# Second layers of the two middle MLP parts as seven half-size products each, in one stream with the first layers

## The chip, the cores and the metric

The kernel runs on one core of one Trainium2 chip. The metric is the device time of one execution in microseconds. A core has five engines that work beside each other and wait for one another through semaphores: TensorE (PE) for matrix products, whose results go to PSUM; VectorE (DVE) and ScalarE (ACT), which read and write both PSUM and SBUF; GpSimd (POOL), which works on SBUF; and SyncE (SP), whose queue issues the transfers from and to HBM. Each engine takes its instructions in a fixed order.

## The reference, cut to what matters

One layer of an encoder for 512 prompt tokens and 64 sample tokens (576 in all), width 1024. After attention, a convolution and an output projection, an MLP with a hidden width of 4096 ends the layer; only this MLP is touched here.

```python
h = rms_norm(x, norm2_g) * (1 + sc2) + sh2
x = x + g2 * (jnp.square(jax.nn.relu(h @ w_ff1)) @ w_ff2)
...
y_prompt = rms_norm(yp, final_g)
y_sample = rms_norm(ys, final_g)
```

`w_ff1` is 1024 x 4096, `w_ff2` 4096 x 1024, all in 32-bit floats.

## The kernel before

**Number format.** A 32-bit operand is split into a high part of the type that TensorE multiplies and a low part, the rest: ACT copies the high part (`copy_to`, L106) and DVE or POOL subtracts it from the source for the low part (`sub`, L115, and L334 in `split`). One product of 128 x 128 weights with a block of tokens is three matmuls: high times high, high times low, low times high. Tokens are columns, in two halves of 288 (`JS`).

**Parts.** The hidden width is cut into four parts of 1024. For each part the first layer makes eight hidden tiles (`a`, 128 hidden rows x 576 tokens, a high and a low part each), and the second layer adds their product with 1024 rows of `w_ff2`, times the gate, onto the residual `x1` (`residual`, L1085, on DVE, straight from PSUM). Part 0's first layer is plain and also prepares the normed input; the last part's second layer is plain as well, in token ranges of 320 and 256, with the final norm behind it.

**Fast first layers.** Parts 1, 2 and 3 make their first layer with Strassen's scheme (`fast_layer`, L1371). Two hidden tiles at a time (a *pair*, `q`), the 2 x 2 blocks of weights (inner half by hidden tile) and of the input (inner half by token half) need seven half-size products instead of eight. The seven moving operands (`op`: "11", "12", "22" and four sums "s1" to "s4") are made once, during part 0's second layer (`operands`, L1294). The seven weight operands (a *block* each, 128 x 512 high and low in one buffer) are made afresh for each pair: `sums` (L1334) forms the sums of weight blocks on DVE, `block` (L1342) copies the high part on ACT and subtracts the low part on DVE (numbers 1, 4, 5) or POOL (0, 2, 3, 6). Blocks go through four buffers and are made three products ahead. A product is 12 matmuls of 288 columns. Products 0 and 2 add up in one PSUM bank, products 1, 3 and 5 in a second and 4 and 6 in a third, and the four results are formed from these banks with a few additions of DVE as the products come: `y` keeps product 0 (ACT), `u` is bank 1 + `y` after product 1, the second `y` the same after product 3, and so on. Because a later product adds onto a bank that is read in between, product 2 must wait until `y` has read bank 0, product 3 for `u`, product 5 for the second `y` and product 6 for the addition from bank 4 (L1417). `made` (L1364) then applies relu and square on ACT, in PSUM, and splits the result into `a`.

**Plain second layers.** For parts 0, 1 and 2 eight output tiles times two token halves times eight hidden tiles times three matmuls (`weight2`, `group`, `residual`; L1488 to L1503). Weights come 128 columns at a time, 512 KB a transfer, and are split by ACT and POOL.

**What sets the order.** PE, ACT, DVE and POOL run in the order in which the code emits their instructions in this stage (`manual_schedule`); the DMA queue is ordered by the scheduler. PSUM has eight banks: two (`tp`) for sums of weights and six that `p_ff` (L1233) hands out in turn. `owed` and `settle` (L1203) put a subtraction off until something later on DVE. `fetch` (L318) issues the next weight transfer, into one of three buffers (`wraw`) or a `spare` one.

Of the kernel before, what the change touches and what calls it, by code (L numbers as in the profile page):

```python
# [71 lines left out]
def step_kernel(ctx: ExitStack, tc: tile.TileContext, io):  # L72
# [240 lines left out]
    for part in range(NP_):  # L313
        order += [f_rows(w_ff1, 0, 128 * (KP * part + m)) for m in range(KP)]
        order += [f_rows(w_ff2, 128 * KP * part, 128 * m) for m in range(NK)]
    stay = []

    def fetch(home=None):  # L318
        if order:
            raw = home() if home else wgt.tile([128, 1024], FT, name="wraw", tag="wraw", bufs=3)  # L320
            src = order.pop(0)
            nc.sync.dma_start(raw.rearrange("p (k c) -> p k c", k=src.shape[1]), src)
            raws.append(raw)
# [1000 lines left out]


    pairs, blocks = {}, {}

    def bring(q):
        b0, b1 = raws.pop(0), raws.pop(0)
        x = p_tp()  # L1330
        copy_to(act, x, b1[:, :512])
        pairs[q] = [b0[:, :512], b0[:, 512:], b1[:, :512], b1[:, 512:], x]

    def sums(q, n):  # L1334

        if n == 2:
            pairs[q].append(p_tp())
        b11, b21, b12, b22, x, *y = pairs[q]
        out, u, v = ((b12, b22, x), (x, x, b11), (y and y[0], b22, x), (y and y[0], b21, y and y[0]))[n]
        sub(dve, out, u, v)  # L1340

    def block(g):  # L1342
        q, b = g // 7, g % 7
        b11, b21, b12, b22, x, y = pairs[q] if len(pairs[q]) == 6 else pairs[q] + [None]
        src = (b11, y, b21, b12, x, y, b22)[b]
# [3 lines left out]
        return lambda: sub(dve if b in (1, 4, 5) else pool, w[:, 1], src, f(w[:, 0]))  # L1349

    MOVING = ("11", "s2", "12", "s3", "s1", "22", "s4")

    def early(n):

        if n == 0:
            bring(0)
            sums(0, 0)
            sums(0, 1)
        else:
            sums(0, 2)  # L1360
            for g in range(2):
                block(g)()

    def made(q, a, r):  # L1364

        act.activation(q, q, AF.Relu)
        act.activation(q, q, AF.Square)
        copy_to(act, a[:, 0, r], q)
        owed.append(lambda: sub(dve, a[:, 1, r], q, f(a[:, 0, r])))

    def fast_layer():  # L1371
        a_ = []
        end = 7 * (KP // 2)
        bk = old = None
        for g in range(end + 2):
            q, s = g // 7, g % 7
            if s == 0:
                old, bk = bk, {}
            if g < end:
                if s in (0, 1, 4):  # L1380
                    bk[s] = p_ff()[:, :HALF]
                t = bk[(0, 1, 0, 1, 4, 1, 4)[s]]
                w, x = blocks.pop(g), ops[MOVING[s]]
                for k in range(4):
                    c = slice(128 * k, 128 * k + 128)
                    r = slice(HALF * (k % 2), HALF * (k % 2) + HALF)
                    for n, (z, y) in enumerate(((0, 0), (0, 1), (1, 0))):
                        pe.matmul(t, lhsT=w[:, z, c], rhs=x[k // 2][:, y, r], start=s in (0, 1, 4) and k + n == 0,  # L1388
                                  stop=k == 3 and n == 2, skip_group_check=True)
            if s == 1 and g < end:  # L1390
                bk["y"] = mt([128, 2, HALF], FT, "y3")
                copy_to(act, bk["y"][:, 0], bk[0])
            todo = [block(h) for h in ((2, 3) if g == 0 else (g + 3,)) if h < end]
            if s == 0 and old:
                dve.tensor_tensor(old[4], old[4], old["u"], op=OP.add)
                settle()
# [203 lines left out]
```

## Time and profile before

| | us |
|---|---|
| median of 3 runs | 837.2 (837.08 to 838.21) |
| the profiled execution | 837.84 |
| its span, first to last instruction | 836.1 |
| PE busy in the span | 784.3 (94%) |
| DVE busy | 526.7 (63%) |
| ACT busy | 465.2 (56%) |
| POOL busy | 296.8 (36%) |

The mean granted clock of TensorE was 0.977 of full speed. The MLP's second half looks like this in time (us from the span's start): the first fast layer begins at 534.7; fast layer and plain second layer of part 1 end at 630.2, those of part 2 at 725.5; part 3's fast layer ends at 769.8 and its second layer, with the final norm and the output, fills the rest. Busy times are unions: where one instruction begins before the one ahead on its engine is through, as on ACT and DVE here, the durations of the instructions add up to more than the busy time.

### The profile page before, as it was taken

Reading aid. Unit: us, or ns where it says so; the run is one execution under the profiler, and the core shown is the slowest. Engines: PE = TensorE matmul, PEld = TensorE weight load, DVE = VectorE, ACT = ScalarE, POOL = GpSimd, SP = SyncE. Lnnn points to the kernel's source line nnn. Section 1 sums busy time; section 2 is a strip of 40 time slices with the busy share of each in tenths; the row PEclk is TensorE's granted clock in tenths of the full one; section 3 lists DMA queues with packets and bytes.
Section 4 is the critical chain, followed back from the end, with each engine's and each line's share of the span. In section 5 each row is a group of like instructions: output and inputs, shape, how many; then the busy total and the mean of one; then the engine's idle time right before and its main releaser. Section 6 shows DMA issues by size and latency. Waiting matters only on the chain.

```text
span 836.1 us, 17187 instructions
## 1 busy us (share of the span) xinstructions
PE 784.3 (94%) x6643; PEld 729.7 (87%) x6643; DVE 526.7 (63%) x1234; ACT 465.2 (56%) x1104; POOL 296.8 (36%) x327
## 2 busy tenths in 40 slices
PE   4898898897889899999999999999999999999995
PEld 3697886486778788898999999999999999999995
DVE  4569879999998444464774678675226731476452
ACT  5354653555676688855465854486216741388231
POOL 1146253131244523323233354444334444344400
PEclk9799999899999999999999999999999999999999
DMA  8974248147434334654132235223322252323311
GB/s 240 322 199 118 77 115 224 53 110 193 116 90 120 93 109 116 201 164 119 52 101 60 81 89 150 79 77 101 101 77 83 55 141 77 88 69 98 101 62 53
DMA packets 164556, 95.57 MB, mean 114 GB/s; under 512 B 7699, under 2 KB 161119, under 8 KB 164475
## 3 DMA queue, kind: packets, MB, share of 16 engines
q1 hardware_dynamic: 164475, 94.48, 40.4%
q8 instruction: 52, 0.85, 0.4%
q14 instruction: 29, 0.24, 0.1%
HBM read 88.82 MB, written 5.64 MB: 113 GB/s over the span
## 4 chain that ended last, share of the span: by engine, by line
PE 67%; DVE 18%; ACT 7%; issue 4%; DMA 2%; POOL 1%; SPq 0%; ACTq 0%; DVEq 0%; POOLq 0%
PE ps_acc L290 9%; PE ps_acc L291 8%; PE ps_acc L292 8%; PE ps_acc L1388 8%; PE ps_lg L1388 4%; DVE yc L566 4%; PE ps_lg L290 3%; PE ps_lg L292 3%; PE ps_lg L291 3%; DVE score L692 3%; DVE m L690 2%; PE ps_av L1388 2%; PE ps_tp L234 2%; PE ps_av L292 2%; PE ps_av L290 2%
## 5 line engine op out<-in xcount | busy, mean ns | idle before, releaser
L334 POOL TENSOR_TENSOR wlo<-wraw,whi 128x512 fp32r<-128x512 f32 x122 | 162.6, 1351 | 271.1 <-ACT whi L106 268.4
L106 ACT ACTIVATE whi<-wraw 128x512 fp32r<-128x512 f32 x148 | 87.6, 624 | 99.5 <-issue 85.3
L290 PE MATMUL ps_acc<-h,whi 128*128 128x288 f32 (+1 forms) x416 | 133.7, 322 | 0.0
L291 PE MATMUL ps_acc<-h,whi 128*128 128x288 f32 (+1 forms) x416 | 124.4, 299 | 0.0
L292 PE MATMUL ps_acc<-h,wlo 128*128 128x288 f32 (+1 forms) x416 | 124.2, 299 | 0.0
L290 PEld LDWEIGHTS ps_acc<-h,whi 128*128 128x128 f32 x416 | 80.0, 192 | 14.3 <-issue 12.7
L291 PEld LDWEIGHTS ps_acc<-h,whi 128*128 128x128 f32 x416 | 80.0, 192 | 0.9
L292 PEld LDWEIGHTS ps_acc<-h,wlo 128*128 128x128 f32 x416 | 79.8, 192 | 0.0
L1089 DVE SCALAR_TENSOR_TENSOR x<-ps_acc,mod,x 128x288 f32<-128x288 f32 (+3 forms) x91 | 36.2, 421 | 60.4 <-PE ps_acc L292 60.0
L566 DVE SCALAR_TENSOR_TENSOR yc<-u,cw,yc 128x606 f32<-128x606 f32 x60 | 58.6, 985 | 0.6
L292 PE MATMUL ps_acc<-a,wlo 128*128 128x288 f32 x192 | 56.6, 295 | 0.0
L290 PE MATMUL ps_acc<-a,whi 128*128 128x288 f32 x192 | 56.6, 295 | 0.0
L291 PE MATMUL ps_acc<-a,whi 128*128 128x288 f32 x192 | 56.6, 295 | 0.0
L749 ACT ACTIVATE gc<-sful,sg 128x544 bf16<-128x544 f32 x48 | 35.8, 745 | 28.6 <-DVE sg L747 27.8
L115 POOL TENSOR_TENSOR whi<-wraw,whi 128x512 fp32r<-128x512 f32 x24 | 31.1, 1295 | 52.3 <-ACT whi L106 51.1
L115 POOL TENSOR_TENSOR wlo<-wraw,wlo 128x512 fp32r<-128x512 f32 x24 | 31.1, 1294 | 34.4 <-ACT wlo L106 32.5
L874 POOL TENSOR_SCALAR prob<-prob,mx 128x128 f32<-128x128 f32 (+3 forms) x32 | 20.2, 634 | 56.8 <-DVE mx L873 31.4
L1388 PE MATMUL ps_acc<-op,whi 128*128 128x288 f32 x264 | 38.5, 295 | 0.0
L1388 PE MATMUL ps_acc<-op,wlo 128*128 128x288 f32 x264 | 38.5, 295 | 0.0
L292 PE MATMUL ps_lg<-a,wlo 128*128 128x288 f32 x128 | 37.8, 295 | 0.0
L291 PE MATMUL ps_lg<-a,whi 128*128 128x288 f32 x128 | 37.7, 295 | 0.0
L290 PE MATMUL ps_lg<-a,whi 128*128 128x288 f32 x128 | 37.7, 295 | 0.0
(418 smaller groups left out, 2267.8 us busy)
## 6 DMA issues: line engine op xcount, KB each, us to landing
wraw<-w_ff SPq DMA_DIRECT2D x64, 512.0 KB
ada<-w_ada SPq DMA_DIRECT2D x44, 512.0 KB
wraw<-w_in SPq DMA_DIRECT2D x24, 512.0 KB
wraw<-w_out SPq DMA_DIRECT2D x8, 512.0 KB
rep<-ud SPq DMA_DIRECT2D x24, 115.0 KB
xtok<-x_prompt SPq DMA_DIRECT2D x4, 512.0 KB
ada<-w_ada SPq DMA_DIRECT2D x8, 256.0 KB
ct<-cache_k SPq DMA_DIRECT2D x8, 256.0 KB
```

The source lines that it names most:

```text
L106: act.activation(out, in_, AF.Copy, scale=1.0 if scale is None else scale)
L115: eng.tensor_tensor(out, a, b, op=OP.subtract)
L290: pe.matmul(out, lhsT=hi, rhs=src[:, 0, cs_], start=first, stop=False)
L291: pe.matmul(out, lhsT=hi, rhs=src[:, 1, cs_], start=False, stop=False)
L292: pe.matmul(out, lhsT=lo, rhs=src[:, 0, cs_], start=False, stop=last)
L334: behind[0] = (second[0] if c.start else pool).tensor_tensor(lo[:, c], raw[:, c], f(hi[:, c]), op=OP.subtract).ins
L566: dve.scalar_tensor_tensor(yc[c], src, w, yc[c], op0=OP.mult, op1=OP.add)
L692: last[0] = dve.match_replace(score[i], m, score[i], SENT).ins
L749: act.activation(eq, sful, AF.Sign, bias=cands[:, z:z + 1], scale=-1.0, accum_out=cnts[:, z:z + 1])
L874: pool.tensor_scalar(pt[:, :n], pt[:, :n], m[:, 1:2], 1.0, op0=OP.mult, op1=OP.mult)
L1089: dve.scalar_tensor_tensor(xm[:, a:b], t[:, a - r.start:b - r.start], mod[:, g, s, m:m + 1], xm[:, a:b], op0=OP.mult, op1=OP.add)
L1388: pe.matmul(t, lhsT=w[:, z, c], rhs=x[k // 2][:, y, r], start=s in (0, 1, 4) and k + n == 0, stop=k == 3 and n == 2, skip_group_check=True)
```

## The change

The second layers of parts 1 and 2 are made with seven half-size products as well. With the tiles of the hidden layer taken as pairs (the two hidden tiles of a pair are the two inner halves) and output tiles as pairs too, a layer has four pairs of seven products. Five layers now form one stream of products, `KINDS`: first and second of part 1 ("in", "out"), first and second of part 2, first of part 3. `line` is the order of the products, `due` a table of what each engine does during which product, `g`, sorted by a rank; `perform(g)` emits it behind the matmuls of product `g`.

The moving operands of an "out" layer are the seven blocks and sums of the squared hidden values. They are made by the "in" layer ahead of it as each pair's results leave PSUM (`evac`, `summed`): four results, of which "21" is needed only inside sums, then the sums "s1" to "s4" by DVE, and seven splits (`opa`) where there were four (`a`). Two small buffers hold values on the way (`va`, `vb`). The "in" layer of part 3 makes `a` as before. The copy `y` of product 0 moves from ACT to DVE in the "in" layers and stays on ACT in the "out" layers. In the "out" layers results go onto the residual (`onto`), eight whole or cut pieces a pair as before. In all five layers two of the four sums of weights (`sum1`, `sum3`) move from DVE to POOL, and with `sum1` in SBUF (`wsum`) also the low part of block 4: POOL has seven instructions a pair where it had four. PSUM banks are handed out by the longest free (`get_bank`, `put_bank`). The last pair of an "in" layer uses smaller delays (`hurry`), and the first two pairs of an "out" layer are interleaved (`line`), so that products come in the order in which their moving operands are made. A 512 KB transfer of `w_ff2` for these layers is issued as two of 256 KB.

```diff
+    for n, (kind, part) in enumerate(KINDS):
+        o = PAIRS * n
+        if kind == "out":
+            line += [(o, 0), (o + 1, 0), (o, 2), (o, 1), (o, 4), (o, 3), (o + 1, 2), (o, 5), (o, 6),
+                     (o + 1, 1), (o + 1, 4), (o + 1, 3), (o + 2, 0), (o + 1, 5), (o + 1, 6)]
+            line += [(o + 2, b) for b in range(1, 7)] + [(o + 3, b) for b in range(7)]
+        else:
+            line += [(o + q, b) for q in range(PAIRS) for b in range(7)]
...
+    def sum1(q):
+        bring(q)[2] = ft_([128, 512], FT, "wsum")
+        sub(pool, pairs[q][2], half_of(q, 2), half_of(q, 0))
...
+    def sum3(q):
+        b12 = half_of(q, 2)
+        sub(pool, b12, half_of(q, 3), b12)
...
-        return lambda: sub(dve if b in (1, 4, 5) else pool, w[:, 1], src, f(w[:, 0]))
+        return lambda: sub(dve if b in (1, 5) else pool, w[:, 1], src, f(w[:, 0]))
...
+    for h, (q, b) in enumerate(line):
+        g = h - 3 if h != 2 else 0
+        block_at(g, h)
+        if b == 1:
+            at(h - 6, 0, sum1, q)
+            at(h - 5, 8, sum2, q)
+            at(h - 4, 8, sum2, q)
+        if b == 3:
+            at(h - 5, 0, sum3, q)
+        if b == 5:
+            at(h - 6, 8, sum4, q)
...
+        def rise(key):
+            act.activation(k_[key], k_[key], AF.Relu)
+            act.activation(k_[key], k_[key], AF.Square)
+            if summed and key == 0:
+                k_["a"] = small_("va")
+                copy_to(act, k_["a"], k_[0])
...
+            def high():
+                if summed:
+                    to.extend(into(o, i))
...
+                copy_to(act, to[0], k_[key])
+
+            def low():
+                sub(dve, to[1], k_[key], f(to[0]))
...
+        def keep():
+            k_["y"] = mt([128, 2, HALF], FT, "y3")
+            copy_to(dve if kind == "in" else act, k_["y"][:, 0], k_[0])
...
+        def sums():
+            add(k_[5], k_[5], k_["b"])
+            sub(dve, k_["a"], k_[5], k_["a"])
...
+            if summed:
+                at(g + 2 + h, 4, sums)
+                at(g + 3 + h, 4, lambda: sub(dve, k_[0], k_[0], k_["b"]))
+                for o, key, d, e in (("s2", "a", 3 + h, h), ("s1", 5, 3 + h, 1), ("s3", 0, 4, h)):
+                    pieces(d, 5, key, o, e)
+        if b == 6:
+            at(g + 1, 0, lambda: add(k_[4], k_[4], k_["u"]))
+            result(1 + h, 4, "12")
+            if summed:
+                at(g + 3 + 3 * h, 7, lambda: sub(dve, k_[4], k_[4], k_["a"]))
+                pieces(4 + 3 * h, 5, 4, "s4")
...
-    for part in range(NP_ - 1):
-        a_ = fast_layer() if part else first_layer()
...
+    a_ = []
+    for n in range(len(KINDS)):
+        fast(PAIRS * n, a_ if n == len(KINDS) - 1 else None)
```

**TensorE, end of part 1's first layer.** `op` is a moving operand of the first layer, `opa` one made from hidden values, `a` a hidden tile; `whi` and `wlo` are weight buffers (in the fast layers a whole block stands in either). Before:

```order
L1388 MATMUL ps_acc<-op,wlo 128x288 x12
L1388 MATMUL ps_acc<-op,whi 128x288 x12
L1388 MATMUL ps_acc<-op,wlo 128x288 x12
L290 MATMUL ps_lg<-a,whi 128x288
L291 MATMUL ps_lg<-a,whi 128x288
L292 MATMUL ps_lg<-a,wlo 128x288
```

Now, from the last two products of the first layer on:

```order
L1479 MATMUL ps_acc<-op,whi 128x288 x12
L1479 MATMUL ps_lg<-op,wlo 128x288 x12
L1479 MATMUL ps_av<-opa,whi 128x288 x12
L1479 MATMUL ps_acc<-opa,wlo 128x288 x12
L1479 MATMUL ps_av<-opa,whi 128x288 x12
L1479 MATMUL ps_lg<-opa,wlo 128x288 x12
L1479 MATMUL ps_acc<-opa,whi 128x288 x12
```

Behind the first layer stand products of 12 matmuls in place of groups of 24, and the third of them adds onto the bank of the first.

**ACT, a middle pair of part 1's first layer**, from the copy of block 1's high part on. L1366/L1496 is relu, L1367/L1497 square, `y_` the copy of product 0 (its buffer numbers differ). Before:

```order
L106 ACTIVATE whi<-ps_tp 128x512
L1366 ACTIVATE ps_acc<-ps_acc 128x288
L1367 ACTIVATE ps_acc<-ps_acc 128x288
L106 ACTIVATE a<-ps_acc 128x288
L106 ACTIVATE wlo<-ps_tp 128x512
L106 ACTIVATE ps_tp<-wraw_7052 128x512
L106 ACTIVATE whi<-wraw_6906 128x512
```

Now:

```order
L106 ACTIVATE wlo<-ps_tp 128x512
L1496 ACTIVATE ps_acc<-ps_acc 128x288
L1497 ACTIVATE ps_acc<-ps_acc 128x288
L106 ACTIVATE va<-ps_acc 128x288
L106 ACTIVATE opa<-ps_acc 128x288
L106 ACTIVATE whi<-wraw 128x512
L1496 ACTIVATE ps_acc<-ps_acc 128x288
L1497 ACTIVATE ps_acc<-ps_acc 128x288
L106 ACTIVATE opa<-ps_acc 128x288
L106 ACTIVATE opa<-ps_lg 128x288
L106 ACTIVATE wlo<-wraw_6845 128x512
```

Between one block and the next, ACT now has up to four 288-wide instructions where it had at most three, or three and the copy `y`.

**DVE, middle pairs of part 1's first layer.** L1395 to L1421 and L1493 are additions, L115 a subtraction; `a<-...,a` and `opa<-...,opa` make a low part. Before, from the second `y` of a pair on (L1413):

```order
L1413 TENSOR_TENSOR y_6978<-ps_lg,y_6978 128x288
L115 TENSOR_TENSOR a<-ps_lg,a 128x288
L115 TENSOR_TENSOR ps_tp<-wraw_6906,ps_tp 128x512
L1417 TENSOR_TENSOR ps_acc<-ps_acc,y_6978 128x288
L115 TENSOR_TENSOR wlo<-ps_tp,wlo 128x512
L1421 TENSOR_TENSOR ps_lg<-ps_lg,y_6978 128x288
```

Now, from the copy of a pair's product 0 (L110) to its second `y`, in the last row:

```order
L110 COPY y_7143<-ps_av 128x288
L1493 TENSOR_TENSOR ps_acc<-ps_acc,vb 128x288
L115 TENSOR_TENSOR va<-ps_acc,va 128x288
L1493 TENSOR_TENSOR u_7173<-ps_acc,y_7143 128x288
L115 TENSOR_TENSOR opa<-ps_lg,opa 128x288
L115 TENSOR_TENSOR ps_acc<-ps_acc,vb 128x288
L115 TENSOR_TENSOR wlo<-ps_tp,wlo 128x512
L115 TENSOR_TENSOR opa<-va,opa 128x288
L115 TENSOR_TENSOR opa<-ps_acc,opa 128x288 x2
L1493 TENSOR_TENSOR y_7143<-ps_acc,y_7143 128x288
```

The second `y`, for which product 5 waits, now stands behind three low parts of sums, of which the first reads SBUF alone.

## Rows read from the trace of the kernel before

**Rows 1.** the page: busy time, share and instructions of each engine in the span

```profile
PE 784.3 (94%) x6643; PEld 729.7 (87%) x6643; DVE 526.7 (63%) x1234; ACT 465.2 (56%) x1104; POOL 296.8 (36%) x327
```

**Rows 2.** busy time by stretch: window, length, busy us (instructions) of each engine, clock, DMA

```profile
core 0: us, PE busy (x) PEld busy (x) DVE busy (x) ACT busy (x) POOL busy (x), PEclk, DMA share, GB/s
...
534.89:579.50 44.61, 44.61 (x340) 44.61 (x339) 30.90 (x60) 34.76 (x80) 20.69 (x16) 1.00 0.26 73
579.50:630.25 50.75, 50.75 (x385) 50.75 (x384) 12.57 (x30) 11.21 (x22) 19.09 (x15) 1.00 0.36 103
630.25:674.80 44.55, 44.55 (x339) 44.55 (x339) 30.84 (x60) 34.82 (x80) 20.66 (x16) 1.00 0.26 73
674.80:725.53 50.73, 50.73 (x386) 50.73 (x385) 12.61 (x30) 11.26 (x22) 19.09 (x15) 1.00 0.37 103
725.53:772.00 46.47, 46.47 (x352) 46.47 (x352) 31.48 (x63) 36.51 (x84) 20.72 (x17) 1.00 0.31 89
```

**Rows 3.** all waits of PE from 530 to 780 us: total, times, longest

```profile
PE ps_av L292 <- POOL wl L334: 0.4, 1, 0.4
```

**Rows 4.** timeline, part 2's fast layer, PE: start, length, engine, line, operation, shapes

```profile
641.19 1.75 PE L1388 MATMUL ps_acc<-op,wlo 128*128 128x288 f32 x12
...
642.78 1.75 PE L1388 MATMUL ps_acc<-op,whi 128*128 128x288 f32 x12
...
649.12 1.75 PE L1388 MATMUL ps_acc<-op,whi 128*128 128x288 f32 x12
```

**Rows 5.** timeline, the same stretch, ACT

```profile
641.20 0.41 ACT L106 ACTIVATE a<-ps_lg 128x288 fp32r<-128x288 f32 x1
...
641.50 0.62 ACT L106 ACTIVATE whi<-wraw 128x512 fp32r<-128x512 f32 x1
...
642.02 0.40 ACT L1366 ACTIVATE ps_av<-ps_av 128x288 f32<-128x288 f32 x1
...
642.46 0.40 ACT L1367 ACTIVATE ps_av<-ps_av 128x288 f32<-128x288 f32 x1
...
642.89 0.41 ACT L106 ACTIVATE a<-ps_av 128x288 fp32r<-128x288 f32 x1
643.19 0.41 ACT L106 ACTIVATE y<-ps_acc 128x288 f32<-128x288 f32 x1
```

**Rows 6.** timeline, the same stretch, DVE; in brackets its idle time before

```profile
644.30 0.68 DVE L115 TENSOR_TENSOR wlo<-ps_tp,wlo 128x512 fp32r<-128x512 f32 x1
...
644.90 0.45 DVE L1407 TENSOR_TENSOR u<-ps_acc,y 128x288 f32<-128x288 f32 x1
...
645.29 0.46 DVE L115 TENSOR_TENSOR a<-ps_lg,a 128x288 fp32r<-128x288 f32 x1
...
649.32 0.47 DVE L1417 TENSOR_TENSOR ps_av<-ps_acc,y 128x288 f32<-128x288 f32 x1 [0.16 <-PE ps_acc L1388]
```

**Rows 7.** timeline, the same stretch, POOL

```profile
642.20 1.29 POOL L115 TENSOR_TENSOR whi<-wraw,whi 128x512 fp32r<-128x512 f32 x1 [0.39 <-ACT whi L106]
```

**Rows 8.** groups of ACT in part 2's fast layer: total us, mean ns, idle before

```profile
L106 ACT ACTIVATE whi<-wraw 128x512 fp32r<-128x512 f32 x9 | 5.5, 628 | 2.8 <-PE ps_acc L1388 1.5 <-PE ps_acc L291 1.3
...
L106 ACT ACTIVATE a<-ps_acc 128x288 fp32r<-128x288 f32 x7 | 2.9, 412 | 0.2
L1366 ACT ACTIVATE ps_acc<-ps_acc 128x288 f32<-128x288 f32 x7 | 2.8, 405 | 0.0
L1367 ACT ACTIVATE ps_acc<-ps_acc 128x288 f32<-128x288 f32 x7 | 2.8, 395 | 0.2
```

**Rows 9.** DVE instructions with two SBUF inputs: min/median/max ns

```profile
L115 DVE TENSOR_TENSOR op<-full,op x16: 448/452/1557, 494.8 to 519.8; 128x288 fp32r<-128x288 f32 x16
L115 DVE TENSOR_TENSOR op<-sums,op x12: 446/456/1554, 496.7 to 524.6; 128x288 fp32r<-128x288 f32 x12
```

**Rows 10.** timeline, part 0's second layer, such instructions beside POOL

```profile
522.77 3.38 DVE L115 TENSOR_TENSOR op<-sums,op 128x288 fp32r<-128x288 f32 x3
...
522.84 3.01 POOL L334 TENSOR_TENSOR wlo<-wraw,whi 128x512 fp32r<-128x512 f32 x2 [3.35 <-ACT whi L106]
```

More of the change, by code (lines that the diff above doesn't have):

```diff
@@ L321, in fetch @@
             src = order.pop(0)
-            nc.sync.dma_start(raw.rearrange("p (k c) -> p k c", k=src.shape[1]), src)
+            if not isinstance(src, list):
+                src = [src]
+            w = 1024 // len(src)
+            for e, v in enumerate(src):
+                nc.sync.dma_start(raw[:, w * e:w * e + w].rearrange("p (k c) -> p k c", k=v.shape[1]), v)
             raws.append(raw)
@@ L1323, in operands, with spare @@
             yield
+    def spare():
+        return ft_([128, 1024], FT, "wraw2")
     pairs, blocks = {}, {}
-    def bring(q):
[L1329 to L1340, printed above, removed]
+    KINDS = [("in", 1), ("out", 1), ("in", 2), ("out", 2), ("in", 3)]
@@ L1351, in step_kernel, with last_split @@
+    for q in range(len(KINDS) * PAIRS):
+        at(7 * q + 1, 9, fetch)
+        if q < len(KINDS) * PAIRS - 2:
+            at(7 * q + 1, 9, fetch, spare)
+    def last_split():
+        second[0] = dve
+        split()
+        second[0] = pool
+    at(END - 2, 9, last_split)
     MOVING = ("11", "s2", "12", "s3", "s1", "22", "s4")
+    opa = {}
     def early(n):
[L1355 to L1362, printed above, removed]
@@ new lines, in small_, with into, fast @@
+    def small_(name):
+        return ffp.tile([128, HALF], FT, name=name, tag="va", bufs=2)
+    def into(o, i):
+        if i % 2 == 0:
+            opa[o, i // 2] = ft_([128, 2, TOK], FR, "opa")
+        c = slice(HALF * (i % 2), HALF * (i % 2) + HALF)
+        x = opa[o, i // 2]
+        return x[:, 0, c], x[:, 1, c]
+    def fast(first, a_=None):
+        kind, part = KINDS[first // PAIRS]
+        bk = [{} for _ in range(PAIRS)]
+        g0 = 7 * first
+        for g in range(g0, g0 + 7 * PAIRS):
+            Q, b = line[g]
+            i = Q - first
+            k_ = bk[i]
+            if b in (0, 1, 4):
+                get_bank(k_, b)
+            t = k_[(0, 1, 0, 1, 4, 1, 4)[b]]
+            w = blocks.pop(g)
+            for k in range(4):
+                c = slice(128 * k, 128 * k + 128)
+                r = slice(HALF * (k % 2), HALF * (k % 2) + HALF)
+                x = ops[MOVING[b]][k // 2] if kind == "in" else opa[MOVING[b], k // 2]
+                for n, (z, y) in enumerate(((0, 0), (0, 1), (1, 0))):
+                    pe.matmul(t, lhsT=w[:, z, c], rhs=x[:, y, r], start=b in (0, 1, 4) and k + n == 0,
+                              stop=k == 3 and n == 2, skip_group_check=True)
+            evac(g, b, i, k_, kind, a_, kind == "in" and i == PAIRS - 1)
+            perform(g)
```

200 lines of the change are left out of this document (115 added, 85 removed).

## The prediction

> **What bounds the kernel now.** I read the page first: PE is busy for 94% of the span, the next, DVE, for 63% [rows 1]. The table by stretch then says where this is strict. From 534.9 us to 725.5 PE is busy for the whole of every stretch, at the full clock of 2.4 GHz (1.00), while DVE and ACT are busy for 69 to 78% of the fast layers and 22 to 25% of the plain second layers [rows 2]. The list of waits agrees: between 530 and 780 us PE waited once, for 0.4 us, at the start of part 3's second layer [rows 3]. So in this stretch time is the number of matmuls times their spacing, and nothing else. The spacing comes from the timeline: products of 12 matmuls start at 641.19 and 642.78, and five products after the first at 649.12 [rows 4], so a product takes 7.93 / 5 = 1.586 us and a matmul 132 ns. A plain second layer of 8 x 2 x 8 x 3 = 384 matmuls takes 384 x 0.1321 = 50.7 us, which is the length of the two stretches in question [rows 2].
>
> **What is removed.** The two second layers become 4 x 7 products of 12 matmuls: 336 each in place of 384. Two layers save 96 matmuls, 96 x 0.132 = **12.7 us**. All of it lies on the path, since PE was never late there. It stays only if PE is still never late, and that is the real question, since the work moves to engines that had room.
>
> **What is added, engine by engine.** I take one middle pair of a first layer whose results are summed (seven products, 11.1 us of PE). Durations overstate the cost here: on ACT the copy that starts at 641.20 lasts 0.41 us, but the next instruction starts 0.30 later; a 512-wide copy lasts 0.62 and holds ACT 0.52; only relu and square, each of which reads what the one before wrote, cost 0.43 or so [rows 5]. On DVE a 512-wide instruction holds the engine 0.60 us and a 288-wide one 0.39 [rows 6].
> - ACT: 34.8 / 4 = 8.7 us a pair before [rows 2]. Seven high parts instead of four and the copy `va`, less the copy `y`: three more, 0.9 us. 9.6 of 11.1.
> - DVE: 30.8 / 4 = 7.7 before. Three 512-wide instructions go (two sums and block 4's low part), -1.8; eight 288-wide come (three low parts, four sums, the copy `y`), +3.1. 9.0 of 11.1.
> - POOL: 20.7 / 4 = 5.2 before; three more at 1.29 [rows 7]. 9.0 of 11.1, one instruction in each product's 1.586.
>
> In the second layers ACT and DVE have about 4.4 and 6.6 us of work a pair. No engine is over PE's pace on average. What remains is order, and I walked the queues by hand over one pair.
>
> **Inside a pair.** ACT's work lies unevenly: beside the seven products it has about 1.9, 2.0, 1.3, 1.7, 1.4, 1.0 and 0.5 us, so it falls behind by at most 0.35 + 0.4 = 0.75 us and has caught up by the pair's end. A block is made three products ahead, 4.76 us; behind by 0.75, with a start 0.2 after the product (DVE starts 0.2 after the next product's first matmul, 649.12 to 649.32 [rows 4, 6]), 0.63 for the copy and 1.29 on POOL, it is there after 2.9. That is hidden. Four times a pair PE waits for DVE with one product, 1.586 us, to cover it: `y`, `u`, the second `y` and the sum from bank 4. Each needs 0.2 + 0.47 = 0.67 us, so DVE may be late by 0.9. The worst is the second `y`, now queued behind three low parts, the last of which waits for ACT's copy of "s3", ACT being behind. In the walk that queue clears about 0.15 us after the product is done: hidden, with some 0.75 to spare. If ACT's copies cost their full length [rows 8], the pair takes 7 x 0.62 + 0.6 + 16 x 0.41 = 11.5 us of ACT, 0.4 more than PE, and the spare is used up after two pairs.
>
> **Two SBUF inputs.** Of the added DVE instructions one a pair, the low part of "s2" from `va`, reads SBUF alone. Such instructions take 0.45 us as a rule and up to 1.56 [rows 9]; in the long cases POOL was at work: three of them took 3.38 us beside two POOL instructions of 3.01, where each pair would take about 2.6 alone [rows 10, 7]. In the walk it falls into a gap of POOL; hit, it costs up to 1.1 and makes the second `y` late by 0.3 to 0.4.
> The Trainium skill (SBUF — State Buffer, section "SBUF: two separate sides") makes this a rule: a VectorE instruction with two SBUF inputs and a GpSimd instruction that reads SBUF share a port pair that one holds for its whole length while the other stands still. By that rule, which the trace bears out with 1.56 against 0.45 us, the moved sums would cost twice, as POOL is now busy four fifths of the time; it speaks against this change and is the second rival below.
>
> **From a first into its second layer.** This place has no row of its own. Beside the last product of the layer and the first of the next, ACT has about 2.0 and 2.5 us to do in 1.586 each, and is some 1.3 us behind when the copy `y` of the new layer's first product comes up. That copy, on ACT here, ends about 0.3 us after the product in between, and the third product must wait for it. On DVE `u` of the second pair of banks is then ready with nothing to spare. I bound this by 0 (the covers hold) and by 1.3 a place (ACT's whole delay lands on PE), and take 0.5, near the walk: two places, **+1.0 us**. From a second into a first layer nothing is behind; no cost. The weights come earlier in the program than before and the doubled number of issues moves the same bytes; the only wait, 0.4 us at part 3's second layer [rows 3], hangs on the copies behind the last product and stays.
>
> **The sum.** 837.84 (the profiled execution) - 12.7 + 1.0 = 826.1. The median of the runs lies 0.6 below that execution, so I predict **825.5 us**.
>
> **Rivals.**
> 1. *ACT sets the pace of the summed layers.* For it: 9.6 of 11.1 leaves little, and full durations give 11.5. Against: rows that start 0.30 after a 0.41-long one. Price: 0.4 x 8 pairs = 3.2, with 0.9 a place at the two changes of layer instead of 0.5, +0.8: 829.5 us.
> 2. *POOL and DVE block each other.* For it: [rows 9, 10]; POOL goes from 46% to 81%. Against: one such instruction a pair, with 0.75 to spare. Price: 8 x 0.35 = 2.8: 828.3 us.
> 3. *Slower than before: DVE and ACT in lockstep.* Every low part waits for its high part, every relu for a sum; where both engines run late together, all four waits of PE in a pair come late. It decides once DVE is more than 0.9 us behind throughout, and is slower than before once each of the eight summed pairs loses over 12.7 / 8 = 1.6 us. At 0.5 for each of four waits it is 16 us: 840.5 us. Against: the addition at 649.32 had waited 0.16 us, and for PE, not for ACT [rows 6], and DVE keeps 2 us free a pair.
> 4. *The matmuls go and the time doesn't*, because PE then waits for weights: 1 MB a pair every 11.1 us is 94 GB/s, and the stretches ran at 73 to 103 [rows 2]. I see no place; about 836.
>
> **How the numbers follow.** Forecast (824.3 to 827.5) 0.63; first rival 0.17, second 0.10, third 0.07, fourth 0.03. The range takes in the case without any wait (837.2 - 12.7 = 824.5, less 0.4 for the spread of runs) and the first two rivals with some room: 824.1 to 831.0. It leaves out the third and fourth. 0.2% (1.7 us) is about what a measurement of this kernel can tell from no change. Faster 0.88: the first three cases, less a little; same 0.05: the fourth, and the mild end of the third; slower 0.07.
>
> **What would show it.** If right: PE busy without a gap from 534.7 to about 712, each of the four layers 44.4 us long, at full clock, DVE and ACT at 80 to 88% of the summed layers, and waits of PE, if any, at the third to sixth product of a second layer, on ACT's `y` or DVE's `u`. First rival: PE waits for high parts or for the second `y` in each later pair, with ACT busy without idle time. Second: instructions `opa<-va,opa` over 1 us long, and PE waits right behind them. Third: summed layers above 51 us. What would make me wrong is a queue I walked too kindly: a wait of ACT in the middle of a pair that pushes all behind it.

## The result, and the profile after

| | before | after |
|---|---|---|
| median, first comparison (4 runs each), us | 837.7 (837.1 to 838.8) | 828.1 (825.8 to 828.8) |
| ratio, 95% interval | | 0.988 (0.986 to 0.990) |
| median, repeated (23 and 4 runs), us | 839.0 (836.2 to 840.6) | 827.0 (826.4 to 829.1) |
| ratio, 95% interval | | 0.987 (0.984 to 0.989) |

By the medians the kernel is 9.6 us faster in the first comparison and 12.1 us in the second. The profiled execution of after took 828.81 us, with a span of 827.0. First the page (busy time of each engine in the span), to be held against [rows 1]:

```profile
PE 772.8 (93%) x6547; PEld 717.6 (87%) x6547; DVE 567.2 (69%) x1336; ACT 492.6 (60%) x1164; POOL 377.2 (46%) x389
```

96 matmuls and 11.5 us of PE are gone, and DVE, ACT and POOL have 40, 27 and 80 us more. By layer of the stream (window, length, busy us and instructions of each engine, clock, DMA), as in [rows 2]:

```profile
536.86:581.29 44.43, 44.43 (x339) 44.43 (x337) 33.43 (x73) 36.85 (x86) 35.70 (x28) 1.00 0.33 94
581.29:626.38 45.09, 44.90 (x338) 44.67 (x337) 33.34 (x72) 23.86 (x47) 36.56 (x30) 1.00 0.33 95
626.38:670.81 44.43, 44.43 (x339) 44.43 (x337) 33.54 (x73) 36.34 (x85) 35.15 (x28) 1.00 0.34 96
670.81:715.88 45.07, 44.89 (x338) 44.65 (x337) 33.31 (x72) 23.86 (x47) 36.53 (x30) 1.00 0.33 94
715.88:760.32 44.44, 44.44 (x339) 44.44 (x338) 26.27 (x53) 33.25 (x75) 32.70 (x27) 1.00 0.22 64
```

The three first layers take what they took, 44.43 us each. The second layers take 45.1 where they took 50.9 (in the trace of before, by the first product of each layer, 579.16 to 630.09 and 674.51 to 725.37). These are all waits of PE from the start of the stream to part 3's second layer (total, times, longest), where [rows 3] had none inside the layers:

```profile
PE ps_av L1479 <- ACT y L106: 0.2, 1, 0.2
PE ps_lg L1479 <- ACT y L106: 0.2, 1, 0.2
```

Each stands at the third product of a second layer. PE's timeline there (start, length, operation, in brackets the idle time before it and who ended it), and the copy `y` on ACT that it waits for:

```profile
582.88 1.75 PE L1479 MATMUL ps_acc<-opa,wlo 128*128 128x288 f32 x12
584.82 1.86 PE L1479 MATMUL ps_av<-opa,whi 128*128 128x288 f32 x12 [0.19 <-ACT y L106]
586.52 1.75 PE L1479 MATMUL ps_lg<-opa,wlo 128*128 128x288 f32 x12
588.11 1.77 PE L1479 MATMUL ps_acc<-opa,whi 128*128 128x288 f32 x12
```

```profile
584.36 0.41 ACT L106 ACTIVATE y<-ps_av 128x288 f32<-128x288 f32 x1
```

The steps between starts are 1.94, 1.70 and 1.59 us. Against 1.59 each, the wait took 0.35 + 0.11 = 0.46 us, though only 0.19 is shown as idle. (A product is shown as 1.75 us long while the next begins 1.59 after its start when nothing is late, so the idle time shown starts 0.16 late.)

From the start of the stream to part 3's second layer, before took 769.79 - 534.73 = 235.06 us and after 760.32 - 536.86 = 223.46: **11.6 us less**. But the stream began 2.1 us later, behind matmuls that are the same in both, and what follows it took 66.7 us in place of 66.3. Whether those 2.1 us belong to the change was the first thing to test. The 0.4 us look like part of it: what follows the stream took 66.7 or 66.8 us in eleven of the twelve profiles of changed kernels below (66.4 in *same_moving*) and 66.3 in both of the kernel before. Less than 0.2 of them lie in TensorE's products there; where the rest comes from stays open.

### The profile page after: what moved, and what is told of

Same layout as the page of the kernel before. It is cut to its first block, busy times and chain, and to the rows that moved or that the text cites. A ratio compares the mean times of both kernels' runs of the same rounds, so it can differ in the third digit from the quotient of the medians.

```text
span 827.0 us, 17314 instructions
## 1 busy us (share of the span) xinstructions
PE 772.8 (93%) x6547; PEld 717.6 (87%) x6547; DVE 567.2 (69%) x1336; ACT 492.6 (60%) x1164; POOL 377.2 (46%) x389
## 4 chain that ended last, share of the span: by engine, by line
PE 67%; DVE 16%; ACT 8%; issue 4%; DMA 2%; POOL 1%; SPq 0%; ACTq 0%; DVEq 0%; POOLq 0%
PE ps_acc L1479 11%; PE ps_lg L1479 9%; PE ps_acc L290 7%; PE ps_acc L291 7%; PE ps_acc L292 7%; PE ps_av L1479 5%; DVE yc L575 3%; DVE score L701 3%; DVE m L699 2%; PE ps_tp L234 2%; PE ps_lg L290 2%; PE ps_lg L291 2%; PE ps_lg L292 2%; DMA ada<-w_ada 1%; ACT gc L758 1%
## 5 line engine op out<-in xcount | busy, mean ns | idle before, releaser
L343 POOL TENSOR_TENSOR wlo<-wraw,whi 128x512 fp32r<-128x512 f32 x92 | 125.5, 1382 | 218.6 <-ACT whi L106 218.3
L115 POOL TENSOR_TENSOR whi<-wraw,whi 128x512 fp32r<-128x512 f32 x42 | 54.5, 1297 | 22.1 <-ACT whi L106 21.9
L1098 DVE SCALAR_TENSOR_TENSOR x<-ps_acc,mod,x 128x288 f32<-128x288 f32 (+4 forms) x96 | 37.5, 415 | 31.0 <-PE ps_acc L292 29.9
L115 POOL TENSOR_TENSOR wlo<-wraw,wlo 128x512 fp32r<-128x512 f32 x38 | 49.3, 1296 | 19.2 <-ACT wlo L106 18.8
L1479 PEld LDWEIGHTS ps_acc<-op,wlo 128*128 128x128 f32 x288 | 39.4, 188 | 0.0
L106 ACT ACTIVATE wlo<-wraw 128x512 fp32r<-128x512 f32 x38 | 24.1, 635 | 15.2 <-PE ps_lg L1479 6.5
L525 PE MATMUL ps_av<-rep,wd 128*32 128x202 f32 x384 | 25.4, 368 | 7.6 <-ACT yc L528 6.7
L1479 PE MATMUL ps_acc<-opa,whi 128*128 128x288 f32 x204 | 29.9, 295 | 0.0
L234 PE MATMUL ps_tp<-ada,cs 128*32 128x128 f32 (+1 forms) x672 | 29.2, 314 | 0.5 <-DMA ada<-w_ada 0.5
L1479 PEld LDWEIGHTS ps_acc<-opa,whi 128*128 128x128 f32 x204 | 28.0, 188 | 0.0
L1479 PE MATMUL ps_lg<-op,wlo 128*128 128x288 f32 x192 | 28.0, 295 | 0.0
```

The costliest lines, as they stand in the source:

```text
L106: act.activation(out, in_, AF.Copy, scale=1.0 if scale is None else scale)
L115: eng.tensor_tensor(out, a, b, op=OP.subtract)
L234: pe.matmul(t[r:r + 32, :w], lhsT=cs[:, 4 * kh + kk, :], rhs=operand(v, kh, kk), start=kk == 0, stop=kk == 3, tile_position=(0, r))
L343: behind[0] = (second[0] if c.start else pool).tensor_tensor(lo[:, c], raw[:, c], f(hi[:, c]), op=OP.subtract).ins
L525: pe.matmul(t[32 * cg:32 * cg + 32, :CT], lhsT=wd[:, 8 * cg + g, :], rhs=rps[h][:, cg, 4 * g:4 * g + CT], start=g == 0, stop=g == 7, tile_ ...
L1098: dve.scalar_tensor_tensor(xm[:, a:b], t[:, a - r.start:b - r.start], mod[:, g, s, m:m + 1], xm[:, a:b], op0=OP.mult, op1=OP.add)
```

## The experiments

In the table, *start* is the first product of part 1's first layer, *stream* the time from there to part 3's second layer, *lost* the stream's excess over the changed kernel's 223.45. All from one profiled execution each.

| kernel | start | stream | lost | execution |
|---|---|---|---|---|
| before | 534.73 | 235.06 | | 837.84 |
| before_again | 536.34 | 235.06 | | 839.5 |
| after | 536.86 | 223.46 | | 828.81 |
| again | 534.31 | 223.44 | | 826.35 |
| full_count | 534.07 | 236.22 | 12.8 | 838.8 |
| y_first | 535.44 | 223.43 | 0.0 | 827.42 |
| y_s1_first | 535.18 | 223.40 | 0.0 | 827.1 |
| three_first | 537.16 | 223.38 | -0.1 | 829.1 |
| same_moving | 535.04 | 223.18 | -0.3 | 826.35 |
| act_load2 | 536.37 | 224.05 | 0.6 | 828.98 |
| act_load | 534.08 | 234.43 | 11.0 | 837.07 |
| dve_psum | 534.43 | 224.76 | 1.3 | 827.83 |
| dve_sbuf | 536.84 | 226.28 | 2.8 | 831.69 |
| sums_dve | 536.27 | 233.04 | 9.6 | 838.13 |

### Do the 2.1 us ahead of the stream belong to the change?

Both kernels once more, nothing edited. *again*:

> The changed kernel, nothing edited. In its first profile the stream of half-size products began 2.1 us later than the same place before (536.86 against 534.73 us), although nothing ahead of it is edited; from there to the last second layer it took 223.5 us where it took 235.1. My theory: the 2.1 us are a matter of the execution, two halves of about 1 us each, one at 35 us and one at 97 us. It expects that a second profile shows another start, 534 to 537 us, again 223.4 to 223.6 us from there to the last second layer, and a median of 826 to 829. The rival, that the changed program itself is later ahead of the stream (its longer code moves something), expects a start of 536.5 us or more again, and a median of 828 or more.

*before_again*:

> The kernel before, nothing edited, beside the run of the changed one. My theory expects the first product of part 1 anywhere between 534 and 537 us, and 235.0 to 235.2 us from there to part 3's second layer. The rival (the changed program is later by itself) expects a start below 535.2 us, as in the first profile (534.73).

The starts were 534.31 for the changed kernel and 536.34 for the one before: the other way round. Over the 14 profiles the start lies anywhere from 534.07 to 537.16, while the stream repeats within 0.02 us in the two profiles of either kernel. So the 2.1 us belong to the execution, not to the change, and the stream is the sharper measure here. Between the two profiles of the changed kernel the start differs by 2.55 us, and two places make it up. Near 102 us TensorE's mean granted clock was 0.57 of full speed in *after* (mostly 1.2 GHz) and 1.00 in *again* (2.4 GHz), and PE, busy throughout, came through 17 matmuls in place of 27 (1.5 us); near 150 us PE waited 4.8 us for ACT's `yc` in place of 3.1 (1.7 us). Ahead of both, *after* had been 0.6 us earlier. Window and list of waits, first of *after*, then of *again*:

```profile
100.00:104.00 4.00, 4.00 (x17) 3.63 (x17) 2.66 (x5) 1.84 (x4) 0.00 (x0) 0.57 0.03 8
PE ps_av L525 <- ACT yc L528: 4.8, 1, 4.8
```

```profile
100.00:104.00 4.00, 4.00 (x27) 3.71 (x26) 3.20 (x6) 2.60 (x7) 0.00 (x0) 1.00 0.03 8
PE ps_av L525 <- ACT yc L528: 3.1, 1, 3.1
```

What sets either was not followed up. A third difference looks like a source and is none. PE's wait for the indexer's relu, near 97 us, was 3.3 us in eight of the 14 profiles and 4.7 or 4.8 in the other six, though all have the same code there:

```profile
PE ps_lg L633 <- ACT relu L636: 4.7, 2, 3.0
```

```profile
PE ps_lg L633 <- ACT relu L636: 3.3, 2, 1.7
```

In the six, PE came to the wait some 1.5 us sooner, since its clock from 85 to 89 us was 1.00, where it was 0.57 to 0.74 in the eight; the product behind the wait then began no later (98.74 us in *after*, 99.37 in *again*). With the clock goes the order of two instructions near 90 us. The timelines of DVE and POOL, first in *after*, then in *again*:

```profile
90.77 1.78 DVE L640 SCALAR_TENSOR_TENSOR score<-relu,wsc,score 128x512 f32<-128x512 f32 x1
```

```profile
90.06 3.64 POOL L343 TENSOR_TENSOR wlo<-wraw,whi 128x512 fp32r<-128x512 f32 x2 [5.76 <-ACT whi L106]
```

```profile
91.27 0.75 DVE L640 SCALAR_TENSOR_TENSOR score<-relu,wsc,score 128x512 f32<-128x512 f32 x1
```

```profile
92.11 1.29 POOL L343 TENSOR_TENSOR wlo<-wraw,whi 128x512 fp32r<-128x512 f32 x1 [7.30 <-ACT whi L106]
```

The score, a DVE instruction with two SBUF inputs, met POOL's subtraction in the first and took 1.78 us; in the second it came ahead of it and took 0.75.

### Is the saving the count of matmuls, and nothing else?

*full_count*:

```diff
+            if kind == "out" and b == 6:
+                for k in range(4):
+                    ...
+                        pe.matmul(t, lhsT=w[:, z, c], rhs=opa["s4", k // 2][:, y, r], start=False, ...
             evac(g, b, i, k_, kind, a_, kind == "in" and i == PAIRS - 1)
```

> In both second layers the last product of each pair is issued twice, so its term is added twice: 8 products of 12 matmuls in place of 7 for each pair, which is the number of matmuls of the plain second layers, 384 each, while all the other work of the change stays. My theory (in this stage time is the number of matmuls by 132 ns, and the moved work costs nothing else) expects 8 x 1.59 = 12.7 us more than the changed kernel, 840 to 842, with the second layers 6.3 us longer. The rival (part of the time of the second layers is waits for the other engines, which a longer stream would swallow) expects less than 12 us more.

The stream took 236.22 us, 12.8 more than 223.45, and the two second layers, by layer (columns as above):

```profile
578.50:629.98 51.48, 51.28 (x386) 51.05 (x385) 33.87 (x72) 23.89 (x47) 37.33 (x30) 1.00 0.29 84
674.41:725.82 51.41, 51.22 (x386) 50.98 (x385) 33.85 (x72) 23.92 (x47) 37.26 (x30) 1.00 0.29 83
```

They are 6.40 and 6.34 us longer, and the waits are the same two. The 96 matmuls are worth 12.7 us, all of it on the path. The median was 840.6 us, 1.002 (1.001 to 1.004) of before: with the count of matmuls of before the change is a small loss, 1.2 us of it in the stream, mostly the waits at the two changes of layer, and 0.4 behind it.

### Can the two waits be taken away?

*y_first* puts the copy `y` ahead of relu, square and high part of result "12" in ACT's queue:

```diff
-            at(g + 1, 0, keep)
+            at(*((g, 2.2) if kind == "out" and i == 0 else (g + 1, 0)), keep)
-            result(1 + h, 4, "12")
+            result(1 + h, 4, "12", 2.5 if summed and hurry else 2)
```

> Only ScalarE's order at the two changes from a first into its second layer is edited: the copy y of the new layer's first product goes ahead of relu, square and high part of the last result of the old one. In the changed kernel this copy ended at about 584.77 us, and the third product began at 584.82 where 584.47 was due, and the next one 0.12 late again: 0.47 us a place. My theory (the copy alone is late) expects no wait of TensorE at either place, second layers of 44.6 us in place of 45.1, and 0.9 us less between the start of the stream and the last second layer, 222.5. The rival (the wait moves to the next thing that is late, the operand 12 that is now copied 0.3 later, or s2 behind it) expects a wait at the third or fourth product of 0.1 to 0.5 us, and 223.0 or more.

The rival holds. PE no longer waits for `y`, and loses as much two products later (waits in the stream, then the timelines of PE, DVE and POOL):

```profile
PE ps_acc L1479 <- DVE opa L115: 0.4, 2, 0.2
```

```profile
586.58 1.87 PE L1479 MATMUL ps_acc<-opa,whi 128*128 128x288 f32 x12 [0.20 <-DVE opa L115]
```

```profile
584.24 1.32 DVE L115 TENSOR_TENSOR opa<-va,opa 128x288 fp32r<-128x288 f32 x1
585.48 0.68 DVE L115 TENSOR_TENSOR ps_tp<-wraw,ps_tp 128x512 f32<-128x512 f32 x1
586.08 0.81 DVE L115 TENSOR_TENSOR opa<-ps_acc,opa 128x288 fp32r<-128x288 f32 x2
```

```profile
583.95 1.29 POOL L115 TENSOR_TENSOR whi<-wsum,whi 128x512 fp32r<-128x512 f32 x1 [1.50 <-ACT whi L106]
```

The low part of "s2" reads SBUF alone, met POOL's block and took 1.32 us in place of 0.45; the low part of "s1", for which PE waits, stands behind it and behind a sum of weights. *y_s1_first* takes that sum out of its way:

```diff
-                for o, key, d, e in (("s2", "a", 3 + h, h), ("s1", 5, 3 + h, 1), ("s3", 0, 4, h)):
+                for o, key, d, e in (("s2", "a", 3 + h, h), ("s1", 5, 3 + h, h), ("s3", 0, 4, h)):
```

> y_first with one edit more. There the wait had moved from the third to the fifth product of each second layer, 0.2 us shown and 0.36 late, for the low part of operand s1: VectorE made it only after the low part of s2, which stood 1.32 us beside a GpSimd instruction of 1.29 instead of 0.45, and after a 512-wide sum for the weights. Here the low part of s1 goes ahead of that sum, 0.6 us earlier. My theory expects no wait of TensorE at either change of layer, second layers of 44.6 us, and 222.5 us from the start of the stream to the last second layer (223.4 with the waits). The rival (a third thing is late behind it, the low parts of the results s3 or s4) expects a wait again and 223.0 or more.

The rival again. The wait went on to the sixth product, and the profile named ACT's copy of a weight block. *three_first* moved that copy ahead:

```diff
-                pieces(4 + 3 * h, 5, 4, "s4")
+                pieces(5 + 2 * h, 5, 4, "s4")
```

> y_s1_first with one edit more. There the wait had moved to the sixth product of each second layer, 0.2 us shown: its weight block's high part stood on ScalarE behind the high part of operand s4, for which ScalarE was idle for 1.15 us until VectorE had the value. Here the high part of s4 (needed only by the ninth product) goes one product later, so the block's copy goes ahead of it: it can start when VectorE's sum ends at about 586.3 us of that trace, 1 us earlier. My theory (each wait has one late instruction, and this is the last of the row) expects no wait of TensorE at either change of layer, second layers of 44.6 us and 222.5 us from the start of the stream to the last second layer. The rival (three engines are full there, and something else is late by as much) expects a wait again and 223.2 or more. In the time of the whole kernel either is 0.9 us or less, under what the rounds can tell.

Nothing changed, the stream took 223.38. In *y_s1_first* PE and DVE read:

```profile
587.93 1.83 PE L1479 MATMUL ps_lg<-opa,wlo 128*128 128x288 f32 x12 [0.21 <-ACT wlo L106]
```

```profile
583.97 1.32 DVE L115 TENSOR_TENSOR opa<-va,opa 128x288 fp32r<-128x288 f32 x1
...
587.34 0.44 DVE L1493 TENSOR_TENSOR u<-ps_lg,y 128x288 f32<-128x288 f32 x1
```

I had believed the name in brackets. But the sixth product adds onto the bank that `u` reads, so the code makes it wait for `u`, which ended at 587.78; the ACT copy that ended beside it feeds a product two places later (the code, not the trace, tells them apart). In both kernels `u` starts 7.73 us after the layer's first product, so *three_first* had moved the wrong instruction. DVE had no gap from 581.65 us up to it, with the 1.32 us of "s2" in between. That the 0.87 us of that collision are what now holds this place is likely and was not tried. The three medians, 827.6, 827.6 and 827.9 us (ratios to before 0.986, 0.987 and 0.987), can't be told from the changed kernel's.

*same_moving* asks whether the operands alone could hold PE up, and why products of second layers are a little slower:

```diff
-                x = ops[MOVING[b]][k // 2] if kind == "in" else opa[MOVING[b], k // 2]
+                x = ops[MOVING[b]][k // 2]
```

> The second layers read the operands of the first layers as their moving side, in place of their own (so they compute another product; all that makes their own operands still runs). Two questions. First, a product of the first layers takes 1.587 us and one of the second layers 1.593, before the change too (a matmul 132.7 ns where 132.2): if that comes from the tiles that are read, it is gone here, and second layers are 0.2 us shorter; if it comes from what the other engines do meanwhile, it stays. Second, TensorE no longer waits for the operands: if the copy y alone is late at the change of layer, its wait of 0.2 us, with 0.47 us lost, stays as it is, 223.1 to 223.4 from the start of the stream to the last second layer; if the operands had held it too, it is less.

The two waits for `y` stayed as they were, 0.20 us each, so `y` is late by itself. The second layers took 44.95 us in place of 45.08: of the 0.18 us that a layer has beyond the 44.43 and the wait, 0.13 went with the tiles that are read, by whatever property of them, or with the waits for their makers, which the products here no longer have; the run doesn't tell the two apart.

### How much room have ACT, DVE and POOL?

*act_load*, six extra copies of ACT in a summed pair, and *act_load2*, two:

```diff
+        if summed and b > 1:
+            for _ in range(1 + (b == 4)):
+                at(g + 1, 1, lambda: copy_to(act, k_["e"], x1[0][:, 0, JS[0]]))
```

> The changed kernel with six extra ScalarE copies (288 wide, of no use) in each of the eight summed pairs. ScalarE was busy for 36.8 of 44.4 us in a summed layer, 9.2 of 11.1 a pair; six copies at 0.34 are 2.0 more: 11.2. My theory (in the changed kernel ScalarE had 1.9 us free a pair, and up to 2 us of lateness is hidden since blocks are made three products ahead) expects summed layers between 44.4 and 45.2 us, and the extra lateness at the change of layer alone: 224 to 228 from the start of the stream to the last second layer. The rival (the order inside the pair decides, not the sum) expects waits in each pair, at the second y or at the blocks, and 231 or more.

> Two extra ScalarE copies a summed pair in place of the six of the run before, which took 11.0 us more. In the middle pairs of a summed layer ScalarE was idle for 0.9 of 11.1 us; two copies take 0.66, six take 2.0. If 0.9 us a pair is the slack, two copies bring no wait inside the pairs, and 0 to 0.6 us more at each change of layer: 223.4 to 224.8 from the start of the stream to the last second layer. If ScalarE's order decides and not its slack, waits show inside the pairs here too, a third of what six brought: 226 to 228.

Six copies cost 11.0 us, so my expectation was far off: I had averaged ACT's idle time over the layer, but most of it lies in the first pair, which has no sums to split yet. The four pairs of part 1's first layer and the first seven products of its second, in *after* (columns as in the layers above):

```profile
536.86:547.97 11.11, 11.11 (x87) 11.11 (x85) 6.40 (x13) 7.02 (x15) 9.19 (x8) 1.00 0.17 49
547.97:559.07 11.10, 11.10 (x86) 11.10 (x85) 9.18 (x21) 9.61 (x24) 8.99 (x8) 1.00 0.33 94
559.07:570.18 11.11, 11.11 (x86) 11.11 (x85) 9.43 (x22) 9.93 (x25) 8.95 (x8) 1.00 0.34 97
570.18:581.29 11.11, 11.11 (x87) 11.11 (x85) 8.43 (x20) 10.29 (x25) 8.57 (x7) 1.00 0.49 137
581.29:592.90 11.61, 11.42 (x86) 11.19 (x85) 10.24 (x22) 8.71 (x21) 9.87 (x9) 1.00 0.17 51
```

ACT was idle for 4.1 us in the first pair and for 1.5, 1.2 and 0.8 in the others; the 0.9 in the expectation of *act_load2* was one of its waits in a middle pair, not all of them. Two copies (0.66) brought no wait inside the pairs, and 0.3 us at each change of layer, as that slack says. The waits with six, then with two:

```profile
PE ps_av L1479 <- ACT y L106: 2.2, 1, 2.2
PE ps_lg L1479 <- ACT y L106: 2.1, 1, 2.1
PE ps_lg L1479 <- DVE y L110: 1.2, 2, 0.6
PE ps_acc L1479 <- DVE y L110: 0.6, 1, 0.6
PE ps_av L1479 <- DVE y L110: 0.6, 1, 0.6
PE ps_acc L1479 <- DVE u L1493: 0.3, 2, 0.2
```

```profile
PE ps_av L1479 <- ACT y L106: 0.5, 1, 0.5
PE ps_lg L1479 <- ACT y L106: 0.5, 1, 0.5
```

*dve_psum* and *dve_sbuf* add three 288-wide additions of DVE to a summed pair at the same places; only the home of one operand differs:

```diff
+        if summed and b in (3, 4, 5):
+            at(g + 1, 0, lambda: dve.tensor_tensor(k_["e"], k_[0], x1[0][:, 0, JS[0]], op=OP.add))
```

```diff
+            at(g + 1, 0, lambda: dve.tensor_tensor(k_["e"], x1[0][:, 1, JS[0]], x1[0][:, 0, JS[0]], op=OP.add))
```

> The changed kernel with three extra VectorE additions in each of the eight summed pairs, each of one operand in PSUM and one in SBUF, 288 wide, 0.39 us of the engine's time: just ahead of the second y, of the sum from bank 4 and of the second row's sum. My theory (these three have 0.9 us to spare: the second y was done at 563.55 in the second profile and its product was due at 564.46) expects no new wait, 223.4 to 224.2 from the start of the stream to the last second layer. The rival (VectorE and ScalarE in lockstep) expects 0.4 us and more a pair, 227 or more.

> The same three extra VectorE additions a pair at the same places, but with both operands in SBUF. My theory (such an instruction can't run beside a GpSimd instruction: 1.32 us in place of 0.45 where the two met in the changed kernel) expects most of the extra ones 0.8 to 1.9 us long, the second y 0.3 us or more too late, and 5 to 16 us more: 228 to 240 from the start of the stream to the last second layer. The rival (the place of the operands doesn't matter, only their time) expects what the additions with a PSUM operand give, 223.4 to 224.2.

The groups of the extra instructions (count, min/median/max ns, first and last start), first two of the three of the run with a PSUM operand, then the one of the run with two in SBUF:

```profile
L1554 DVE TENSOR_TENSOR u<-ps_lg,x x12: 444/446/458, 629.6 to 667.7; 128x288 f32<-128x288 f32 x12
...
L1554 DVE TENSOR_TENSOR u<-ps_av,x x6: 443/450/458, 539.4 to 566.9; 128x288 f32<-128x288 f32 x6
```

```profile
L1554 DVE TENSOR_TENSOR u<-x x24: 440/808/1584, 541.5 to 672.0; 128x288 f32<-128x288 f32 x24
```

With PSUM none of them was ever longer than 0.46 us, POOL busy or not; with SBUF the median was 0.81 and the longest 1.58. PE waited for the second `y` in two pairs of eight in the first case (0.42 us each, the last pair of each layer; 1.3 us lost) and in four in the second (0.43 each; 2.8 lost). Both expectations missed. In the first case I had expected no wait, from the 0.9 us that the second `y` has to spare in every pair of the changed kernel. With the additions it had 0.93, 0.85 and 0.54 us in the first three pairs of part 1 and was late in the fourth: what DVE is late by adds up from pair to pair. In the second case the mechanism is the one expected, the size is not (5 to 16 us): I had let every addition hit POOL and none of the delay be made up, while two fifths took 0.6 us or less, and DVE's gaps took up most of the rest.

*sums_dve* puts the sums of weight blocks back on DVE, which now have two SBUF inputs each:

```diff
-        sub(pool, pairs[q][2], half_of(q, 2), half_of(q, 0))
+        sub(dve, pairs[q][2], half_of(q, 2), half_of(q, 0))
...
-        sub(pool, b12, half_of(q, 3), b12)
+        sub(dve, b12, half_of(q, 3), b12)
```

> The changed kernel with the two sums of weight blocks that it moved to GpSimd put back on VectorE, for all 20 pairs: two 512-wide instructions a pair with both operands in SBUF, 0.69 us alone; GpSimd does five in place of seven. By time alone VectorE would be at 8.4 + 1.2 = 9.6 of 11.1 us in a summed pair. My theory (a VectorE instruction with two SBUF operands stands while a GpSimd instruction runs) expects many of these 40 sums 1 to 2 us long, and waits of TensorE of 0.4 us in about half of the pairs: 226 to 232 from the start of the stream to the last second layer. The rival (only VectorE's time counts, and it has room) expects 223.4 to 224.8.

9.6 us lost, the upper end of my expectation and a little over. By time alone, with 1.2 us more, DVE would have had 0.5 to 0.7 us of room left in the middle pairs, but hardly any in the first seven products of a second layer, where it was busy for 10.2 of 11.6 us. One of the sums' groups on DVE, and PE's longest waits:

```profile
L115 DVE TENSOR_TENSOR wsum<-wraw,wraw x19: 680/1342/1789, 538.4 to 748.8; 128x512 f32<-128x512 f32 x19
```

```profile
PE ps_lg L1479 <- DVE u L1493: 1.2, 2, 1.0
PE ps_av L1479 <- DVE u L1493: 1.2, 2, 1.0
PE ps_lg L1479 <- DVE ps_acc L1493: 1.1, 3, 0.6
PE ps_acc L1479 <- DVE ps_acc L1493: 0.9, 2, 0.6
```

The two waits of 1.0 us stand in those first seven products, so the run doesn't part the collisions from DVE's plain load there. These moves to POOL, which the prediction counted only by their time, are worth three quarters of the saved matmuls against the same sums on DVE with both inputs in SBUF. Sums on DVE with one input in PSUM, as in the kernel before, were not tried in the changed one.

## Why the prediction was right, and where it was not

The time forecast, 825.5 us, is 2.6 us under the first median and 1.5 under the second, and both are in the range. The first, 828.1, lies beyond the narrower 824.3 to 827.5 of the forecast and beside the second rival's 828.3, so the time alone doesn't tell these two apart; the trace does, by the stream and by the waits that are missing inside the pairs.

- **The matmuls.** 12.7 us forecast; *full_count* measures 12.7 (6.40 + 6.34).
- **The change of layer.** +1.0 us forecast, at the third product, for ACT's `y`; 2 x 0.46 = 0.9 measured, at that product, for that copy. The bounds of 0 to 1.3 a place were wide and the walk was near. The stream as a whole: -11.7 forecast, -11.6 measured. (The products of the second layers, 0.2 us a layer slower than those of the first, were so before as well.)
- **Inside the pairs.** No wait in eight summed pairs, as forecast. The spare time of the second `y` was put at 0.75 us; in *again* it ended at 563.55 in a middle pair and its product was due at 564.46, 0.9 later, and in the other seven pairs it was 0.9 as well.
- **The loads.** Forecast for a middle pair: 9.6, 9.0 and 9.0 us for ACT, DVE and POOL. The two middle pairs of part 1 were busy for 9.6 and 9.9, 9.2 and 9.4, 9.0 and 9.0 (the rows under *act_load*), so the counting was right; the fourth pair, 10.3 for ACT, wasn't counted. In the second layers I gave ACT and DVE 4.4 and 6.6; they had 6.0 and 8.3. More than half of that excess lies in the first seven products (8.7 and 10.2), because the last pair's sums and splits fall into them, which is what the change of layer waits for.
- **First rival** (ACT sets the pace): not so, with little to spare. The two copies of *act_load2* still fit, the six of *act_load* did not.
- **Second rival** (POOL and DVE block each other): the collision exists, 1.32 us, at "s2" of the last pair of both layers, as these rows of DVE and POOL in *after* show; in the other six pairs that instruction took 0.45, in a gap of POOL, as the walk had it. It is not the first thing late, but the second, as *y_first* shows.

```profile
585.65 1.32 DVE L115 TENSOR_TENSOR opa<-va,opa 128x288 fp32r<-128x288 f32 x1
```

```profile
585.36 1.29 POOL L115 TENSOR_TENSOR whi<-wsum,whi 128x512 fp32r<-128x512 f32 x1 [1.50 <-ACT whi L106]
```

The Trainium skill (SBUF — State Buffer, section "SBUF: two separate sides") says that such a DVE instruction and a POOL instruction that reads SBUF exclude each other; the runs agree, with 0.45 and up to 1.58 us for one addition by the home of an operand alone. The prediction held this against the change; for the sums with both inputs in SBUF, *sums_dve* has it the other way: on POOL they brought no wait of TensorE inside the pairs, on DVE they took up to 1.79 us each.

- **Third and fourth rival**: no trace of either. (The third's 840.5 starts from 824.5; from 825.5, as in the other rivals, 16 us more are 841.5.)
- **The base**, the mis-sized term. I took the profiled execution, 837.84, and the spread of three runs for firm. The start of the stream alone moved by 3 us between profiles, and the medians of before ran from 837.7 to 839.4 over the comparisons. The sum should have been a difference of stretches that repeat, with 1 to 2 us of spread on the base. For the 0.4 us behind the stream it had no term.

## What to carry to other kernels

Where one engine is never late for 180 us, a saving on it can be read off as count times spacing, and the risk is in the seams: walk the queues of the other engines at each change of phase, by the load of the middle of a phase and not by its average. Behind the first late instruction stand others that are late by as much; taking one away moves the wait on, and the name that a trace gives for it should be held against what the code makes the waiting instruction need. When work moves off a tight engine, look where its operands live: of two additions of the same size on DVE, the one with both inputs in SBUF is the dear one while POOL works. Delays that are hidden in one pair can add up over the next.

## What I had not expected of the hardware

- A wait costs PE about 0.25 us more than the idle time shown: 0.19 shown and 0.46 lost in *after*, 0.42 and 0.66 in *dve_psum*, 0.53 and 0.79 in *act_load2*. Of this, 0.16 is the overlap of 1.75 us long products that begin 1.59 apart; the other 0.1 is the first product after the wait, which takes that much longer.
- A matmul of a second layer is 0.2 to 0.5 ns slower than one of a first, before as after (50.93 and 50.86 us for 384 are 132.6 and 132.4 ns, where a first layer's 44.43 for 336 are 132.2). In the changed kernel most of that went away when other tiles were read; why is not known.
- The same instructions of DVE and POOL, near 90 us, fall in one of two orders from execution to execution, and the order goes with TensorE's granted clock just before: in the six profiles with 1.00 from 85 to 89 us the score met POOL and took 1.78 or 1.79 us, in the eight with 0.57 to 0.74 it went ahead and took 0.74 or 0.75. PE's wait behind them is 4.7 us in the first case and 3.3 in the second, and PE leaves it no later.
